# Attention in a two-layer encoder: division and transposes of a unit one turn later, values two turns later, convolution products moved into later stages

## The chip, the core and the metric

The kernel runs on one core of one Trainium2 chip. The metric is device microseconds (us) of one launch; lower is better. Engines are called by their names: TensorE (PE in the profile; its weight loads are PEld), VectorE (DVE), ScalarE (ACT), GpSimd (POOL) and SyncE (SP), which issues most of the loads.

## The reference

What is computed is an encoder of two layers over a prompt of 512 tokens and a sample of 256 tokens, D = 1024. Each layer is a gated feed-forward part, a mixer, and a second feed-forward part, each followed by a scaled residual and a layer norm. The mixer has one input projection, and two head groups that read it: a windowed attention and a long convolution (Hyena). Cut to the mixer:

```python
z = h @ w_in[l]
q, k, v, hz = jnp.split(z, [D_ATTN, D_ATTN + KV_WIDTH, D_ATTN + 2 * KV_WIDTH], axis=-1)
...
def _window_attention(q, k, v, sink):          # blocks of 128 queries, own block and both neighbours as keys
    s = jnp.einsum('bnqkgd,bnskd->bnkgqs', qb, kb) * (HEAD_DIM ** -0.5)
    s = jnp.where(valid[None, :, None, None], s, -jnp.inf)
    m = jnp.maximum(s.max(-1, keepdims=True), sink_f)
    p = jnp.exp(s - m)
    p = p / (p.sum(-1, keepdims=True) + jnp.exp(sink_f - m))
    o = jnp.einsum('bnkgqs,bnskd->bnqkgd', p.astype(v.dtype), vb)
...
def _bidir_long_conv(u, filt, bias):
    U = jnp.fft.rfft(uf, n=2 * L, axis=1)
    K = jnp.fft.rfft(kern, n=2 * L, axis=0)
    y = jnp.fft.irfft(U * K[None], n=2 * L, axis=1)[:, :L]
...
x <- LN_b(alpha*x + (1+g2)*W_out[RMS(attn_group) | RMS(hyena_group)])
```

There are 8 query heads and 2 key heads of 64, so each key head serves a group of 4 query heads. A block of 128 queries sees two key blocks where it is at an end of its sequence, and three otherwise.

## The kernel before, in words

**Precision and memory.** Every large product is three TensorE products of a high and a low part: high by high, high by low, low by high. Splitting takes a copy (mostly ScalarE, which rounds to the high part) and a subtraction (VectorE, the low part). Buffers are drawn in turn from pools (`SLOTS`, L120): `slot_s` 10, `slot_w` 6, `slot_r` 7, `slot_t` 6, `bank` 8 (the accumulators of TensorE), `tiny` 12. An instruction waits until the last reader of the buffer that it takes over is done.

**Order.** Each engine does its instructions in the order in which the Python code issues them; nothing reorders them later. All of them pass through one recording helper, `call` (L67, its body L70), so every row of the profile says L70, and an instruction is known by its tiles.

**The mixer of a layer** (`run`, L1371). `proj.unit(n)` (L444) is one unit of the input projection, 4 to 11 here. Between them stands the convolution, in two halves of the channels (`hy0`, `hy1`; class `Hyena`, L1275 to L1323). For each half: `u_transposes` (L1244) turns the gated input, `u_spectrum` (L1257) multiplies it with a DFT matrix (36 matmuls, six banks that ScalarE copies out), `products(a)` (L1283) for the thirds a = 0, 1, 2 multiplies with the filter's spectrum on VectorE with splits on ScalarE, `inverse(a)` (L1307) goes back with 24 matmuls, and `gate(a)` (L1321) multiplies the result into `x0` on VectorE. Then come three passes g = 0, 1, 2 over two query groups and the keys with the values, three steps each: 48 matmuls, the transposes of the step before, then on ScalarE and VectorE the rotary step and the splits. After each of the nine steps `side(3 * g + tp)` (L1405) issues pieces of other work: rest of the convolution, the group norm of its output (`Rms`, L1325: squares, stats, bcast, apply), and the start of attention.

**Attention** (`Attention`, L1513). Its work is 12 units, a block of queries times a group of 4 heads: units 0 to 3 the sample's, 4 to 11 the prompt's. Units 6 to 9 have three key blocks (384 columns a head), the others two (256). A unit goes through

- `scores` (L1526): 8 matmuls into banks; VectorE adds the mask and takes the row maxima, one instruction a head, into `slot_w`;
- `exps` (L1552): ScalarE, four exponentials with row sums, and one small one for the sink term;
- `norms` (L1562): VectorE adds the sink term, forms the reciprocal, and divides two heads; ScalarE divides the other two;
- `turned` (L1575): TensorE transposes the probabilities, one bank per key block, and ScalarE copies each bank out as the high part; `turned_lo` (L1588): VectorE forms the low parts (the second parts) from the same banks;
- `values` (L1592): 6 or 9 matmuls, then a ScalarE copy into `oT`.

The loop in `attention` (L1652) runs over turns u = 1 to 12. Unit 0 and the scores and exponentials of unit 1 are issued ahead of it by `side`. Within a turn also stand: `filler` (L1636, 12 in all, 12 matmuls each, the hyena half of the output projection, and its addition to the residual on VectorE), `block_squares` (L1620, a ScalarE square and two VectorE sums for a finished block, for the group norm), and the group norm of the sample. `Out` (L489) takes the output projection's weights; its `ahead` says how many units of weights are split before their turn.

Of the kernel before, what the change touches and what calls it, by code (L numbers as in the profile page):

```python
# [160 lines left out]
def _program(mem, nc, x_in, c_col, c_row, w_units, ada_nat, ada_t, ada_b, ln_p, conv_p, sink_in, grp_in,  # L161
# [1025 lines left out]
    def mixer(l, x_prev, hh, hl):  # L1187
# [183 lines left out]
        def run(end):  # L1371
# [10 lines left out]
            proj.unit(8)  # L1382
            hy0.inverse(0, dinv)
            u_transposes(1)
            hy0.products(2)
            proj.unit(9)
            hy0.gate(0)
            hy0.inverse(1, dinv)
            hy1 = Hyena(1, u_spectrum(1, dfw))
            hy0.gate(1)  # L1390
            hy0.inverse(2, dinv)
            hy1.products(0)
            proj.unit(10)
            hy0.gate(2)
            hy1.products(1)
            proj.unit(11)
            hy1.inverse(0, dinv)
            hy1.products(2)
            hy1.gate(0)

            rms = [Rms(x0[0], 4, s) for s in range(2)]
            on_hy = []
            att = []

            def side(i):  # L1405
                if i == 0:
                    hy1.inverse(1, dinv)
                    hy1.gate(1)
                elif i == 1:
                    hy1.inverse(2, dinv)  # L1410
                    hy1.gate(2)
                    rms[0].squares()
                elif i == 2:
                    rms[1].squares()
                elif i == 3:
                    for r in rms:
# [188 lines left out]
        def attention(at, rms, on_hy, last_q, end):  # L1605
# [14 lines left out]
            def block_squares(qb):  # L1620

                if not Q:
                    Q.append(slot_t([T]))
                cols = slice(qb * P, (qb + 1) * P)
                sq = slot_t([4, P])
                act.activation(out=sq, in_=oT[:, :, cols], func=AF.Square)
                tt(sq[:, 0:2], sq[:, 0:2], sq[:, 2:4], ALU.add)
                tt(Q[0][:, cols], sq[:, 0], sq[:, 1], ALU.add)
# [1 line left out]
            oT = slot_s([4, T])  # L1630
            o_hy = Out([on_parts(on_hy, k) for k in range(4)])
            fill = [(d, ks) for d in range(6) for ks in ((0, 1), (2, 3))]
            share = (0, 0, 1, 1, 1, 1, 1, 1, 1, 1, 1, 2)
            fbank = {}

            def filler():  # L1636
# [12 lines left out]

            on_at, done = [], []  # L1650
            rms_at = [Rms(oT, 0, s) for s in range(2)]
            for u in range(1, 13):  # L1652
                if 1 < u < 12:
                    at.scores(u)
                if u > 1:
                    at.turned(u - 1)
                    if u < 12:
                        at.exps(u)
                else:
                    filler()  # L1660
                    last_q()
                if u > 1:
                    at.turned_lo(u - 1)
                if done:
                    block_squares(done.pop())
                if u == 1:
                    rms[0].apply(on_hy, (2, 3))
                elif u == 2:
                    rms[1].apply(on_hy, (2, 3))
                    reload()  # L1670
                elif u == 6:
                    rms_at[1].Q = Q[0][:, SEQ[1]]
                    rms_at[1].stats()
                elif u == 7:
                    rms_at[1].bcast()
                    on_at.append(slot_s([2, 2, T], F32R))
                elif u == 8:
                    rms_at[1].apply(on_at, (0, 1))
                elif u == 11:
                    on_at.append(slot_s([2, 2, T], F32R))  # L1680
                    rms_at[1].apply(on_at, (2, 3))
                adds = [filler() for _ in range(share[u - 1])]
                if u < 12:
                    at.norms(u)
                for add in adds:
                    add()
                at.values(u - 1, oT)
                if at.units[u - 1][1]:
                    done.append(at.units[u - 1][0])
            block_squares(done.pop())  # L1690
            while fill:
                filler()()
# [233 lines left out]
```

## Time and profile before

| what | value |
|---|---|
| median of 3 runs | 2940.02 us (2939.73 to 2941.28) |
| the profiled execution's own time | 2938.19 us |
| its span in the trace | 2936.2 us |
| mean granted TensorE clock, of full speed | 0.987 |
| busy TensorE, matmuls (PE) | 2837.5 us, 97% of the span |
| busy TensorE, weight loads (PEld) | 2594.4 us, 88% |
| busy VectorE | 2139.2 us, 73% |
| busy ScalarE | 1367.5 us, 47% |
| busy GpSimd | 331.8 us, 11% |
| mean DMA rate | 124 GB/s |

Busy shares are averages over the whole launch, feed-forward parts and mixers together. A mean says nothing of a stage: the mixer of layer 0 lies at about 700 to 960 us of the span, its attention loop at about 863 to 950. The full speed of TensorE's clock is 2.4 GHz, and the lower level 1.2 GHz; a granted clock between 0.5 and 1 is a mean over a stretch with both.

### The profile page before, as it was taken

Reading aid. Unit: us, or ns where it says so; the run is one execution under the profiler, and the core shown is the slowest. Engines: PE = TensorE matmul, PEld = TensorE weight load, DVE = VectorE, ACT = ScalarE, POOL = GpSimd, SP = SyncE. Lnnn points to the kernel's source line nnn. Section 1 sums busy time; section 2 is a strip of 40 time slices with the busy share of each in tenths; the row PEclk is TensorE's granted clock in tenths of the full one; section 3 lists DMA queues with packets and bytes.
Section 4 is the critical chain, followed back from the end, with each engine's and each line's share of the span. In section 5 each row is a group of like instructions: output and inputs, shape, how many; then the busy total and the mean of one; then the engine's idle time right before and its main releaser. Section 6 shows DMA issues by size and latency. Waiting matters only on the chain. (4 is left out here: it accounts for less than half of the span.)

```text
span 2936.2 us, 42164 instructions
## 1 busy us (share of the span) xinstructions
PE 2837.5 (97%) x16468; PEld 2594.4 (88%) x16468; DVE 2139.2 (73%) x3821; ACT 1367.5 (47%) x2355; POOL 331.8 (11%) x394
## 2 busy tenths in 40 slices
PE   9999999999998999999999999999999899999998
PEld 3789999988887889999988999998888788999997
DVE  5788778878967887777588777557896787444558
ACT  3544444444366544444445444444436644444444
POOL 2400000031000300000030000002100030000000
PEclk9999999999999999999999999999999999999999
DMA  5546665542121135664333665344212112455332
GB/s 202 194 171 173 188 176 164 147 151 103 57 73 51 65 127 161 194 194 116 107 122 122 179 176 157 107 107 145 102 63 73 51 57 89 85 115 115 97 108 83
DMA packets 102607, 364.65 MB, mean 124 GB/s; under 512 B 13750, under 2 KB 17031, under 8 KB 99208
## 3 DMA queue, kind: packets, MB, share of 16 engines
q1 hardware_dynamic: 74968, 259.88, 24.5%
q0 software_dynamic: 27440, 102.08, 16.2%
q8 instruction: 129, 2.11, 0.3%
q14 instruction: 70, 0.57, 0.1%
HBM read 284.33 MB, written 80.74 MB: 124 GB/s over the span
## 5 line engine op out<-in xcount | busy, mean ns | idle before, releaser
L70 PE MATMUL bank<-slot_s,slot_w 128*128 128x384 f32 (+2 forms) x13176 | 2322.1, 336 | 44.0 <-DVE slot_s L70 26.7
L70 PEld LDWEIGHTS bank<-slot_s,slot_w 128*128 128x128 f32 x13176 | 2130.5, 190 | 212.2 <-DVE slot_s L70 23.0
L70 DVE TENSOR_TENSOR slot_w<-slot_w,slot_w 128x1024 fp32r<-128x1024 f32 (+2 forms) x444 | 370.0, 864 | 4.1 <-ACT slot_w L70 1.6
L70 DVE CUSTOM_DVE_ANT_0 slot_t<-slot_r,slot_r 128x1024 bf16<-128x1024 f32 x256 | 311.4, 1223 | 77.4 <-DMA x_spill<-slot_t 45.0
L70 ACT ACTIVATE slot_w<-slot_w 128x1024 fp32r<-128x1024 f32 (+1 forms) x298 | 249.7, 838 | 119.2 <-DVE slot_w L70 118.9
L70 DVE TENSOR_TENSOR slot_w<-slot_r,slot_w 128x1024 fp32r<-128x1024 f32 (+1 forms) x194 | 222.0, 1153 | 113.4 <-ACT slot_w L70 111.9
L70 ACT ACTIVATE slot_t<-bank,tiny 128x512 f32<-128x512 f32 (+1 forms) x256 | 147.5, 580 | 307.9 <-PE bank L70 302.1
L70 POOL DMA_DIRECT2D x_spill<-slot_t x128 | 110.4, 862 | 1409.2 <-ACT slot_t L70 1409.2
L70 ACT ACTIVATE slot_w<-slot_r 128x1024 fp32r<-128x1024 f32 (+1 forms) x194 | 189.0, 992 | 155.9 <-DVE slot_r L70 98.1
L70 ACT ACTIVATE slot_t<-slot_t 128x384 f32<-128x384 f32 (+2 forms) x161 | 84.1, 526 | 334.2 <-DVE slot_t L70 334.0
L70 DVE TENSOR_TENSOR slot_t<-bank,slot_t 128x384 f32<-128x384 f32 x228 | 125.5, 555 | 144.2 <-PE bank L70 73.5
L70 DVE TENSOR_TENSOR slot_s<-slot_t,slot_s 128x768 fp32r<-128x768 f32 (+2 forms) x190 | 153.1, 810 | 52.6 <-ACT slot_s L70 48.4
L70 ACT ACTIVATE slot_s<-slot_t 128x768 fp32r<-128x768 f32 (+2 forms) x160 | 113.8, 717 | 159.9 <-DVE slot_t L70 155.5
L70 ACT ACTIVATE slot_t<-bank 128x384 f32<-128x384 f32 (+3 forms) x282 | 139.6, 495 | 101.6 <-PE bank L70 99.1
L70 PE MATMUL bank<-slot_s,slot_r 128*128 128x384 f32 x912 | 172.0, 337 | 0.0
L70 PEld LDWEIGHTS bank<-slot_s,slot_r 128*128 128x128 f32 x912 | 160.6, 188 | 0.0
L70 DVE TENSOR_TENSOR slot_r<-slot_w,slot_r 128x512 fp32r<-128x512 f32 x76 | 52.0, 684 | 106.4 <-ACT slot_r L70 106.4
L70 ACT ACTIVATE slot_t<-slot_s 128x256 f32<-128x256 f32 (+1 forms) x132 | 65.9, 510 | 108.0 <-DVE slot_s L70 104.1
L70 PE MATMUL bank<-slot_w,slot_s 128*128 128x256 f32 x864 | 107.9, 284 | 3.1 <-DVE slot_w L70 1.8
L70 PEld LDWEIGHTS bank<-slot_w,slot_s 128*128 128x128 f32 x864 | 104.7, 191 | 3.9 <-DVE slot_w L70 2.1
L70 DVE SCALAR_TENSOR_TENSOR slot_t<-bank,slot_t 128x384 f32<-128x384 f32 x76 | 42.3, 556 | 83.4 <-PE bank L70 82.2
L70 DVE SCALAR_TENSOR_TENSOR slot_s<-bank,tiny,slot_s 128x256 f32<-128x256 f32 (+1 forms) x160 | 87.0, 564 | 15.1 <-PE bank L70 14.9
(137 smaller groups left out, 2132.2 us busy)
## 6 DMA issues: line engine op xcount, KB each, us to landing
slot_r<-w_units SPq DMA_DIRECT2D x170, 512.0 KB, 4.8
slot_w<-w_units SPq DMA_DIRECT2D x146, 512.0 KB, 4.1
slot_r<-ada_t SPq DMA_DIRECT2D x128, 512.0 KB, 5.8
x_spill<-slot_t POOLq DMA_DIRECT2D x128, 384.0 KB, 5.3
slot_s<-x_spill POOLq DMA_DIRECT2D x12, 1536.0 KB, 8.2
x_spill<-slot_s POOLq DMA_DIRECT2D x10, 1024.0 KB, 4.6
slot_r<-ada_nat SPq DMA_DIRECT2D x16, 512.0 KB, 5.9
g_main<-slot_s POOLq DMA_DIRECT2D x4, 1536.0 KB, 10.0
```

The lines of the kernel that those rows point to most:

```text
L70: return getattr(real, name)(*args, **kwargs)
```

## The change

The attention loop gets 13 turns in place of 12. In turn u it issues: scores (and maxima) of unit u, `norms` of u-1, exponentials of u, other work, fillers, `values` of u-2, `turned` of u-1, the fillers' additions, `block_squares`, and last `turned_lo` of u-1. Before, turn u had scores of u, `turned` of u-1, exponentials of u, `turned_lo` of u-1, `block_squares`, other work, fillers, `norms` of u, additions, `values` of u-1. The group norm of the sample moves by one turn, both applications of the hyena group norm stand at u = 1, and `o_hy.ahead` is 1 in place of 2. In the convolution, `hy0.products(2)`, the units 10 and 11 of the projection, and the second half's inverses, last products and gates are placed anew, some of them into `side` 0 to 2. No instruction's shape is changed.

```diff
@@ run, convolution @@
             u_transposes(1)
-            hy0.products(2)
             proj.unit(9)
             hy0.gate(0)
             hy0.inverse(1, dinv)
             hy1 = Hyena(1, u_spectrum(1, dfw))
             hy0.gate(1)
+            hy0.products(2)
+            proj.unit(10)
+            hy1.products(0)
+            proj.unit(11)
             hy0.inverse(2, dinv)
-            hy1.products(0)
-            proj.unit(10)
             hy0.gate(2)
             hy1.products(1)
-            proj.unit(11)
-            hy1.inverse(0, dinv)
-            hy1.products(2)
-            hy1.gate(0)
...
             def side(i):
                 if i == 0:
+                    hy1.inverse(0, dinv)
+                    hy1.gate(0)
+                elif i == 1:
                     hy1.inverse(1, dinv)
+                    hy1.products(2)
                     hy1.gate(1)
-                elif i == 1:
+                    rms[0].squares()
+                elif i == 2:
                     hy1.inverse(2, dinv)
                     hy1.gate(2)
-                    rms[0].squares()
-                elif i == 2:
                     rms[1].squares()
...
@@ attention @@
-            share = (0, 0, 1, 1, 1, 1, 1, 1, 1, 1, 1, 2)
+            share = (1, 0) + (1,) * 11
...
-            for u in range(1, 13):
+            o_hy.ahead = 1
+            for u in range(1, 14):
                 if 1 < u < 12:
                     at.scores(u)
-                if u > 1:
-                    at.turned(u - 1)
-                    if u < 12:
-                        at.exps(u)
-                else:
-                    filler()
+                if u == 1:
                     last_q()
-                if u > 1:
-                    at.turned_lo(u - 1)
-                if done:
-                    block_squares(done.pop())
-                if u == 1:
-                    rms[0].apply(on_hy, (2, 3))
-                elif u == 2:
-                    rms[1].apply(on_hy, (2, 3))
+                    for r in rms:
+                        r.apply(on_hy, (2, 3))
+                elif u < 13:
+                    at.norms(u - 1)
+                if 1 < u < 12:
+                    at.exps(u)
+                if u == 2:
                     reload()
...
                 adds = [filler() for _ in range(share[u - 1])]
-                if u < 12:
-                    at.norms(u)
+                if u > 1:
+                    at.values(u - 2, oT)
+                if 1 < u < 13:
+                    at.turned(u - 1)
                 for add in adds:
                     add()
-                at.values(u - 1, oT)
-                if at.units[u - 1][1]:
-                    done.append(at.units[u - 1][0])
+                if done:
+                    block_squares(done.pop())
+                if u > 1 and at.units[u - 2][1]:
+                    done.append(at.units[u - 2][0])
+                if 1 < u < 13:
+                    at.turned_lo(u - 1)
```

**ScalarE in the turn of unit 8 (three key blocks), before.** `slot_w` with 384 columns are the probabilities: `slot_w_1092` those of unit 7, `slot_w_1108` those of unit 8. `x4` are exponentials, `x2` a division of two heads, `64x4x128` a copy of values, and `slot_r<-bank` copies of transposed probabilities:

```order
L70 ACTIVATE slot_w_1092_8087<-slot_w_1092_8087,tiny_1093_8088 128x384 x2
L70 ACTIVATE slot_s_1021_7674<-bank_1107_8165 64x4x128
L70 ACTIVATE slot_r_1115_8202<-bank_1114_8197 128x512
L70 ACTIVATE slot_r_1117_8209<-bank_1116_8204 128x512
L70 ACTIVATE slot_r_1119_8216<-bank_1118_8211 128x512
L70 ACTIVATE slot_w_1108_8176,tiny_1109_8177<-slot_w_1108_8176,tiny_1109_8177 128x384 x4
...
L70 ACTIVATE slot_w_1108_8176<-slot_w_1108_8176,tiny_1109_8177 128x384 x2
```

The same place after the change, where `slot_w_1087` is unit 7 and `slot_w_1102` unit 8:

```order
L70 ACTIVATE slot_w_1087_8061<-slot_w_1087_8061,tiny_1088_8062 128x384 x2
L70 ACTIVATE slot_w_1102_8146,tiny_1103_8147<-slot_w_1102_8146,tiny_1103_8147 128x384 x4
...
L70 ACTIVATE slot_s_1021_7674<-bank_1112_8196 64x4x128
L70 ACTIVATE slot_r_1114_8212<-bank_1113_8207 128x512
L70 ACTIVATE slot_r_1116_8219<-bank_1115_8214 128x512
L70 ACTIVATE slot_r_1118_8226<-bank_1117_8221 128x512
L70 ACTIVATE slot_t_1119_8228<-slot_s_1021_7674 128x512
L70 ACTIVATE slot_w_1102_8146<-slot_w_1102_8146,tiny_1103_8147 128x384 x2
```

Behind the division of unit 7 now stand at once the exponentials of unit 8; the copy of values (now those of unit 6), the three copies of the transposed unit 7 and, in this turn, a square come after them, where the copies stood ahead of them.

**VectorE in the same turn, before.** `RECIPROCAL` and `x2` are the division, `ISA` with `mask` a row maximum of one head (three more are left out), `slot_r<-bank,slot_r` the low parts of the transposed unit:

```order
L70 TENSOR_TENSOR tiny_1093_8088<-tiny_1093_8088 128x4
L70 RECIPROCAL tiny_1093_8088<-tiny_1093_8088 128x4
L70 TENSOR_SCALAR slot_w_1092_8087<-slot_w_1092_8087,tiny_1093_8088 128x384 x2
L70 SCALAR_TENSOR_TENSOR slot_s_1018_7669<-bank_1087_8054,tiny_1020_7672,slot_s_1018_7669 128x512
L70 SCALAR_TENSOR_TENSOR slot_s_1018_7669<-bank_1088_8055,tiny_1020_7672,slot_s_1018_7669 128x256
L70 ISA slot_w_1108_8176,tiny_1109_8177<-bank_1110_8178,mask 128x384
...
L70 TENSOR_TENSOR slot_r_1115_8202<-bank_1114_8197,slot_r_1115_8202 128x512
L70 TENSOR_TENSOR slot_r_1117_8209<-bank_1116_8204,slot_r_1117_8209 128x512
L70 TENSOR_TENSOR slot_r_1119_8216<-bank_1118_8211,slot_r_1119_8216 128x512
...
L70 TENSOR_TENSOR tiny_1109_8177<-tiny_1109_8177 128x4
L70 RECIPROCAL tiny_1109_8177<-tiny_1109_8177 128x4
L70 TENSOR_SCALAR slot_w_1108_8176<-slot_w_1108_8176,tiny_1109_8177 128x384 x2
```

After the change:

```order
L70 ISA slot_w_1102_8146,tiny_1103_8147<-bank_1104_8148,mask 128x384
...
L70 TENSOR_TENSOR tiny_1088_8062<-tiny_1088_8062 128x4
L70 RECIPROCAL tiny_1088_8062<-tiny_1088_8062 128x4
L70 TENSOR_SCALAR slot_w_1087_8061<-slot_w_1087_8061,tiny_1088_8062 128x384 x2
L70 TENSOR_TENSOR slot_t_1119_8228<-slot_t_1119_8228 128x256
L70 TENSOR_TENSOR slot_t_1069_7975<-slot_t_1119_8228 128x128
L70 TENSOR_TENSOR slot_r_1114_8212<-bank_1113_8207,slot_r_1114_8212 128x512
L70 TENSOR_TENSOR slot_r_1116_8219<-bank_1115_8214,slot_r_1116_8219 128x512
L70 TENSOR_TENSOR slot_r_1118_8226<-bank_1117_8221,slot_r_1118_8226 128x512
L70 ISA slot_w_1120_8235,tiny_1121_8236<-bank_1122_8237,mask 128x384
```

Before, the division of unit 7 stands ahead of the maxima of unit 8, and the low parts of unit 7 behind them. After, the maxima of unit 8 come first, then the division of unit 7, the sums of a square and the low parts of unit 7, and only then the maxima of unit 9 (`slot_w_1120`).

## Rows read from the trace of the kernel before

Columns are explained with the first group of each view. In the timeline, "idle" is the engine's time without work just before the instruction, and the name behind the arrow is what ended it.

**Rows 1.** Windows of 20 us, layer 0: busy PE, PEld, DVE, ACT, POOL; PEclk, DMA, GB/s.
```profile
860.00:880.00 20.00, 16.48 (x86) 13.41 (x85) 16.58 (x56) 15.93 (x45) 0.00 (x0) 0.83 0.05 19
...
900.00:920.00 20.00, 16.79 (x98) 14.27 (x99) 17.33 (x61) 15.59 (x39) 0.00 (x0) 1.00 0.01 2
```

**Rows 2.** Timeline, convolution, layer 0: start, us, engine, operation, [idle before it <- releaser].
```profile
751.02 0.68 DVE L70 TENSOR_TENSOR slot_r<-slot_r,slot_s 128x512 f32<-128x512 f32 x1
...
752.04 3.04 PE L70 MATMUL bank<-slot_s,slot_w 128*128 128x256 f32 x24
...
754.88 1.47 DVE L70 TENSOR_TENSOR slot_w<-slot_r,slot_w 128x512 fp32r<-128x512 f32 x2
...
759.43 2.53 PE L70 MATMUL bank<-slot_s,slot_w 128*128 128x256 f32 x12 [4.34 <-DVE slot_s L70]
...
765.31 16.84 PE L70 MATMUL bank<-slot_s,slot_w 128*128 128x512 f32 x96
...
796.56 0.47 DVE L70 TENSOR_TENSOR slot_t<-bank,rope 128x32 f32<-128x32 f32 x4
...
797.70 0.90 DVE L70 TENSOR_TENSOR slot_r<-slot_t,slot_r 128x128 fp32r<-128x128 f32 x4 [0.44 <-ACT slot_r L70]
...
801.42 0.81 PE L70 MATMUL bank<-ident,slot_r 128*128 128x128 f32 x8
```

**Rows 3.** Timeline, one turn of attention with three key blocks, DVE and ACT.
```profile
907.77 0.15 DVE L70 TENSOR_TENSOR tiny<-tiny 128x4 f32<-128x4 f32 x1
...
908.23 1.12 ACT L70 ACTIVATE slot_w<-slot_w,tiny 128x384 f32<-128x384 f32 x2 [1.17 <-DVE tiny L70]
...
909.26 0.57 ACT L70 ACTIVATE slot_s<-bank 64x512 f32<-64x512 f32 x1
...
909.89 0.55 DVE L70 CUSTOM_DVE_ANT_0 slot_w<-bank,mask 128x384 f32<-128x384 f32 x1
...
910.33 1.58 ACT L70 ACTIVATE slot_r<-bank 128x512 fp32r<-128x512 f32 x3 [0.49 <-PE bank L70]
...
912.26 1.88 DVE L70 TENSOR_TENSOR slot_r<-bank,slot_r 128x512 fp32r<-128x512 f32 x3
...
912.38 0.62 ACT L70 ACTIVATE slot_w<-slot_w,tiny 128x384 f32<-128x384 f32 x1 [0.47 <-DVE tiny L70]
...
914.79 0.19 ACT L70 ACTIVATE tiny<-tiny 128x4 f32<-128x4 f32 x1
```

**Rows 4.** Timeline, one turn with two key blocks, DVE and ACT.
```profile
872.63 0.91 ACT L70 ACTIVATE slot_w<-slot_w,tiny 128x256 f32<-128x256 f32 x2 [0.87 <-DVE tiny L70]
...
873.11 0.42 DVE L70 CUSTOM_DVE_ANT_0 slot_w<-bank,mask 128x256 f32<-128x256 f32 x1
...
874.95 1.28 DVE L70 TENSOR_TENSOR slot_r<-bank,slot_r 128x512 fp32r<-128x512 f32 x2
...
876.99 0.19 ACT L70 ACTIVATE tiny<-tiny 128x4 f32<-128x4 f32 x1
```

**Rows 5.** Timeline, a square, its sums and a weight split in other turns.
```profile
883.18 0.62 ACT L70 ACTIVATE slot_t<-slot_s 128x512 f32<-128x512 f32 x1
...
883.83 0.75 DVE L70 TENSOR_TENSOR slot_t<-slot_t 128x256 f32<-128x256 f32 x2 [1.50 <-ACT slot_t L70]
...
897.79 1.04 ACT L70 ACTIVATE slot_w<-slot_r 128x1024 fp32r<-128x1024 f32 x1
```

**Rows 6.** Timeline, DVE: the reciprocals of units 1 and 11, the first and last of eleven.
```profile
865.75 0.18 DVE L70 RECIPROCAL tiny<-tiny 128x4 f32<-128x4 f32 x1
...
940.78 0.18 DVE L70 RECIPROCAL tiny<-tiny 128x4 f32<-128x4 f32 x1
```

**Rows 7.** Timeline, PE: two waits ahead of transposes in attention.
```profile
866.46 1.94 PE L70 MATMUL bank<-ident,slot_w 128*128 128x128 f32 x8 [3.05 <-DVE slot_w L70]
...
900.98 1.00 PE L70 MATMUL bank<-ident,slot_w 128*128 128x128 f32 x4 [2.17 <-DVE slot_w L70]
```

**Rows 8.** Timeline, PE: the wait for weights after attention.
```profile
953.31 1.93 PE L70 MATMUL bank<-slot_s,slot_w 128*128 128x256 f32 x14 [0.76 <-DVE slot_w L70]
```

More of the change, by code (lines that the diff above doesn't have):

```diff
@@ L1651, in attention @@
             rms_at = [Rms(oT, 0, s) for s in range(2)]
-            for u in range(1, 13):
+            o_hy.ahead = 1
+            for u in range(1, 14):
                 if 1 < u < 12:
                     at.scores(u)
-                if u > 1:
-                    at.turned(u - 1)
-                    if u < 12:
-                        at.exps(u)
-                else:
-                    filler()
-                    last_q()
-                if u > 1:
-                    at.turned_lo(u - 1)
-                if done:
-                    block_squares(done.pop())
-                if u == 1:
-                    rms[0].apply(on_hy, (2, 3))
-                elif u == 2:
-                    rms[1].apply(on_hy, (2, 3))
+                if u == 1:
+                    last_q()
+                    for r in rms:
[5 more added lines that the diff above has]
+                if u == 2:
                     reload()
-                elif u == 6:
+                elif u == 7:
                     rms_at[1].Q = Q[0][:, SEQ[1]]
                     rms_at[1].stats()
-                elif u == 7:
+                elif u == 8:
                     rms_at[1].bcast()
                     on_at.append(slot_s([2, 2, T], F32R))
-                elif u == 8:
+                elif u == 9:
                     rms_at[1].apply(on_at, (0, 1))
-                elif u == 11:
+                elif u == 12:
                     on_at.append(slot_s([2, 2, T], F32R))
```

## The prediction

> **What bounds the kernel now.** I read the totals first: TensorE is busy for 97% of the span, VectorE for 73%, ScalarE for 47%. Then the busy time by stretches of 20 us: TensorE is full in the feed-forward parts and has its holes in the two mixers. In the attention stretch it works 16.5 and 16.8 us of 20, beside 16 to 17 us of VectorE and 16 us of ScalarE [rows 1]: no engine is full, so the stretch is held by a chain that runs from engine to engine. Then the timeline of the two places that the change touches, in layer 0 (layer 1 shows the same holes some 1,395 us later).
>
> *Convolution.* TensorE stops for 4.34 us at 759.4 [rows 2] in the middle of the spectrum of the second half: the ScalarE copies that free its banks stand behind the copies of `products(2)`, which wait for VectorE. VectorE has no gap from there to the rotary step of the first key pass at 796.56 [rows 2].
>
> *Attention.* One turn with three key blocks goes like this [rows 3]: VectorE adds the sink term at 907.77, ScalarE divides two heads from 908.23, copies the last values at 909.26 and the transposed probabilities at 910.33, VectorE takes the maxima from 909.89 to 912.26, ScalarE the exponentials from 912.38 to 914.98, and the next division follows at once, or after a square or a group norm. VectorE's second parts at 912.26 lie beside the exponentials. The loop that closes is division, maxima, exponentials. From the reciprocal of unit 1 to that of unit 11 there are ten turns in 75.03 us [rows 6].
>
> **The change, part by part.** Durations are those of one profiled execution, 2938.19 us with a span of 2936.2 us; the median of the runs is 1.83 us above it, and I add that at the end. No instruction is added or removed on any engine; only order, and with it tile reuse, changes.
>
> *1. The loop of a turn, the large term.* In the new order ScalarE has: division of unit u-1, exponentials of u, copy of the values of u-2, copies of the turned u-1, square. VectorE has: maxima of u, division of u-1, additions, square sums, second parts of u-1, and only then the maxima of u+1. The second parts need ScalarE's copies, the copies stand behind the exponentials of u, and those need the maxima of u. So everything that lay beside the exponentials is now in one closed loop, which I add up from rows, each duration as the step to the next instruction on its engine.
> With three blocks [rows 3]: maxima 2.37 (909.89 to 912.26), to ScalarE 0.46 (907.77 to 908.23), division 1.03, exponentials 2.50, values copy 0.55, three copies 1.58, last second part 0.65: **9.14 us**. With two blocks [rows 4]: maxima 1.84 (873.11 to 874.95), 0.46, division 0.81 (0.91 less the 0.1 by which neighbours on ScalarE overlap), exponentials 2.08 (from 875.0 to 877.1), 0.55, two copies 1.09 (two thirds of 1.58 and a start), 0.65: **7.48 us**. Where a square falls in the turn, VectorE's square sums wait for ScalarE's square and stand ahead of the second parts, which then can't follow the copies one by one: the copies (1.50 or 1.00), square 0.62, 0.04, sums 0.67, all second parts 1.80 or 1.20 [rows 3, 5] replace the last two terms, which gives **11.54** and **9.27**. A weight split on ScalarE adds 0.95 [rows 5].
> The ten turns u = 2 to 11: four plain ones of two blocks (2, 3, 4, 11) 29.92; u=5 with a square 9.27; u=6, maxima of three blocks but a division of two, with square and split, 11.17; u=7 9.14; u=8 with square 11.54; u=9, where the group norm of the sample adds about 1.2, 10.35; u=10, two and three blocks with square and split, 11.54. Sum 92.93, against 75.03: **+17.9**. The maxima of unit 2 start at about 865.2, 0.4 before the old division of unit 1, and from the end of turn 11 to the last values matmul I count 7.9 us (division, turned copies, square, second parts, values) where there were 8.85: -1.35. TensorE's own work in the three-block turn of that timeline (scores 1.58, transposes 1.53, filler 2.35, values 2.25: 7.7 us) fits into the loop and costs nothing more; if its clock fell, see the second rival. Attention: **+16.55 per layer**.
>
> *2. Weights after attention.* With one split ahead in place of two, the first unit of the attention half of the output projection is split only behind the last values copy and the last square. Copy 0.6, square 0.6, ScalarE's split 1.05 and VectorE's 1.2 make about 3.5 us before its third matmul; now TensorE runs on and waits 0.76 one unit later [rows 8]. The second unit then starts about 6.6 us after the values in place of 3.87: **+2.7 per layer**. Bounds: 0, if the wait is eaten by a later one that stands anyway, and 4.4, if the clock falls in it.
>
> *3. Products later.* VectorE's queue up to the rotary step loses `products(2)` of the second half, 5.35 us like its twin (751.02 to 756.35 [rows 2]), and a gate of 0.65; the queue is full, but it now comes to unit 10's convolution about 2 us before TensorE has finished that unit (8.4 us, half of 16.84 [rows 2]). So the rotary step moves from 796.56 to about 792.5, and the transposes that follow it 2.05 us later (796.56 to 798.60) are ready at 794.5. TensorE, without the old hole, ends the spectrum at 756.6 (36 matmuls from 752.04 at 3.04 us for 24), and with two units 16.84, two inverses of 3.04 and two key passes of 6.1 it is there at 791.7 and waits. In place of 801.42 less the inverse of 3.0 us that it still owes, that is **-3.9 per layer**. Bounds: -6.7, if it does not wait, and 0. `products(2)` and its inverse now stand in the key passes, where VectorE waits for TensorE again; I cost them at nothing, and at 3 us if the inverse of that third has to wait for them.
>
> *4. Queues.* SP's loads keep their order and come tens of us before use; POOL moves one small power. Filler matmuls, 12 as before, one per turn: nothing.
>
> Sum per layer: 16.55 + 2.7 - 3.9 = 15.35; two layers 30.7. 2938.19 + 30.7 + 1.83 = **2971 us**.
>
> **Rivals.** *Slower still: the clock.* In the loop TensorE waits twice a turn, mostly 1.7 to 2 us, but about 3.05 us in u=8, where scores of unit 9 need banks that the second parts of unit 7 still hold. Before, a wait of 2.17 us left the clock at its upper level (1.00 in that stretch), and one of 3.05 us was followed by the lower one: 0.83 as the mean of its 20 us [rows 1, 7]. If it falls in most of the turns 6 to 10, their TensorE work of 7.7 us takes up to 15.4 and becomes the bound: 5 x 15.4 = 77 for 53.7, so up to 23 us per layer, 3017 us at the end. Against it: one fall costs only 2 or 3 us, and part of that is idle anyway. The Trainium skill ("TensorE: Matmul & The Clock Gate", section "A second HAM failure mode: psum-queue depth-cycling") says that TensorE can swing between its levels where it idles briefly between groups of matmuls as it cycles through banks; by that rule the time would be this rival's, and the trace, where a 2.17 us wait did nothing, agrees only for the longer wait.
>
> *Faster: TensorE is the bound.* If dividing a unit late really took ScalarE and VectorE off the path, a turn would last as long as TensorE's own work: scores, transposes, filler and values, 6.1 us with two blocks and 7.7 with three, 67.4 for the ten turns, -7.6; with the whole 6.7 from the convolution 14.3 per layer, **2911 us**. For it: the new order asks for values two turns after the scores. Against it: it needs the copies of u-1 ahead of the exponentials of u on ScalarE, or the maxima of u+1 ahead of the second parts of u-1 on VectorE, and both stand the other way. It would decide as soon as ScalarE's wait for the maxima were gone.
>
> *No change.* The convolution gives 6.7 and attention costs no more: it would need turns of about 8.3 us on average, which only holds if the squares' extra 2 us in five turns, the rest of the copies and the weight wait all vanish: 2940 us.
>
> **Numbers.** Forecast 0.76 (range of its own 2951 to 2992: -6.7, no weight wait and 4.5 us less in the turns at the one end; 0, 4.4 and two clock falls of 2.5 us per layer at the other). Clock rival 0.10, faster 0.08, no change 0.06. I give 2950 to 2994, which leaves out the faster case, no change and the greater part of the clock case. A change under 0.2% (5.9 us) can't be told from none by these runs. Slower: 0.86, same 0.05, faster 0.09.
>
> **What would show it.** In the new trace the ten turns from the maxima of unit 2 to those of unit 12's place should take 90 to 97 us; ScalarE should wait for VectorE ahead of each division and each exponential, and VectorE for ScalarE ahead of the second parts, with TensorE's waits on VectorE's second parts in each turn. The hole at 759 should be gone and a shorter one stand ahead of the transposes of the first key pass. The forecast is wrong if the turns come out near 7 us, or if the second parts of a unit start before the exponentials of the next have ended.

## The result, and the profile after

The changed kernel takes **2973.2 us** (median of 4 runs, 2971.89 to 2974.78) against 2939.88 us before: a ratio of 1.0116, 95% interval 1.0098 to 1.0133. The forecast was 2971 us. The profiled execution took 2971.89 us with a span of 2969.7 us, 33.5 us more than the span before.

The windows of the changed kernel come first: two of 20 us that answer to [rows 1], then the turns of units 3, 6 and 8, each from its first row maximum to the next unit's, and last 5 us behind attention. Columns as in [rows 1].

```profile
860.00:880.00 20.00, 16.61 (x91) 13.40 (x90) 10.79 (x47) 12.39 (x40) 0.00 (x0) 0.91 0.08 27
900.00:920.00 20.00, 15.83 (x79) 12.43 (x79) 11.96 (x41) 11.52 (x31) 0.71 (x1) 0.91 0.00 1
...
866.65:874.11 7.46, 5.72 (x27) 4.53 (x26) 4.97 (x20) 4.42 (x14) 0.00 (x0) 0.79 0.00 0
891.28:902.33 11.05, 6.17 (x25) 4.63 (x23) 6.32 (x22) 6.30 (x16) 0.00 (x0) 0.82 0.00 0
911.85:923.24 11.39, 7.24 (x37) 5.40 (x36) 5.82 (x22) 6.05 (x16) 0.00 (x0) 0.95 0.00 1
...
965.00:970.00 5.00, 5.00 (x25) 5.00 (x25) 2.54 (x5) 0.61 (x2) 0.40 (x1) 0.51 0.88 286
```

VectorE and ScalarE, at 16 to 17 us of 20 before, are down to 11 or 12, and TensorE has not filled the room. No engine is full, which fits three engines that wait for each other in a closed chain; the timeline shows the waits. In the turn of unit 8 TensorE works 7.2 of 11.4 us.

The timeline of the changed kernel, in order of time: the convolution, the turn of unit 3 (two key blocks), the turn of unit 8 (three blocks and a square), and the start of the weights behind attention.

```profile
744.10 2.44 DVE L70 SCALAR_TENSOR_TENSOR slot_s<-bank,convp,slot_s 128x511 f32<-128x511 f32 x4
...
749.26 21.16 PE L70 MATMUL bank<-slot_s,slot_w 128*128 128x256 f32 x132
...
789.22 0.48 DVE L70 TENSOR_TENSOR slot_t<-bank,rope 128x32 f32<-128x32 f32 x4
...
790.58 1.19 PE L70 MATMUL bank<-ident,slot_r 128*128 128x128 f32 x8 [1.66 <-ACT slot_r L70]
...
866.65 0.41 DVE L70 CUSTOM_DVE_ANT_0 slot_w<-bank,mask 128x256 f32<-128x256 f32 x1
...
868.95 1.31 ACT L70 ACTIVATE slot_w<-slot_w,tiny 128x256 f32<-128x256 f32 x3 [3.06 <-DVE tiny L70]
...
872.30 1.06 ACT L70 ACTIVATE slot_r<-bank 128x512 fp32r<-128x512 f32 x2
...
872.91 1.29 DVE L70 TENSOR_TENSOR slot_r<-bank,slot_r 128x512 fp32r<-128x512 f32 x2 [2.35 <-ACT slot_r L70]
...
874.11 0.41 DVE L70 CUSTOM_DVE_ANT_0 slot_w<-bank,mask 128x256 f32<-128x256 f32 x1
...
914.68 1.63 ACT L70 ACTIVATE slot_w<-slot_w,tiny 128x384 f32<-128x384 f32 x3 [3.70 <-DVE tiny L70]
...
918.68 1.54 ACT L70 ACTIVATE slot_r<-bank 128x512 fp32r<-128x512 f32 x3
...
920.11 0.63 ACT L70 ACTIVATE slot_t<-slot_s 128x512 f32<-128x512 f32 x1
920.77 0.75 DVE L70 TENSOR_TENSOR slot_t<-slot_t 128x256 f32<-128x256 f32 x2 [5.39 <-ACT slot_t L70]
921.44 1.88 DVE L70 TENSOR_TENSOR slot_r<-bank,slot_r 128x512 fp32r<-128x512 f32 x3
922.18 1.65 PE L70 MATMUL bank<-slot_s,slot_s 128*128 128x384 f32 x4 [2.74 <-DVE slot_r L70]
...
962.51 0.50 PE L70 MATMUL bank<-slot_s,slot_w 128*128 128x256 f32 x2 [2.29 <-ACT slot_w L70]
963.77 8.47 PE L70 MATMUL bank<-slot_s,slot_w 128*128 128x256 f32 x46 [0.76 <-DVE slot_w L70]
```

*Convolution.* The 4.34 us hole of [rows 2] is gone: TensorE runs through the spectrum and the two units behind it without a wait (749.26; 36 and 96 matmuls). The first rotary step stands at 789.22 in place of 796.56, and a shorter wait, 1.66 us, now stands ahead of the transposes behind it.

*A turn.* ScalarE waits 3.06 us for VectorE's maxima and reciprocal (868.95; the row holds two divisions and the first exponential), does division, exponentials and one copy of values, and copies the transposed unit only at 872.30. VectorE, idle for 2.35 us, can start the second parts only then, and behind them come the next maxima, 7.46 us after the last. In the turn of unit 8, VectorE waits 5.39 us, because the sums of the square wait for ScalarE's square at 920.11 and the second parts stand behind them; TensorE waits 2.74 us at 922.18 for banks that those second parts hold.

*Behind attention.* TensorE stops for 2.29 and 0.76 us at 962.51 and 963.77 for weights, where 0.76 us stood in [rows 8], and its granted clock from 965 to 970 is 0.51.

### The profile page after: what moved, and what is told of

Its sections match the earlier page's. It is cut to its first block, busy times and chain, and to the rows that moved or that the text cites. A ratio compares the mean times of both kernels' runs of the same rounds, so it can differ in the third digit from the quotient of the medians.

```text
span 2969.7 us, 42163 instructions
## 1 busy us (share of the span) xinstructions
PE 2851.7 (96%) x16468; PEld 2603.9 (88%) x16468; DVE 2139.3 (72%) x3821; ACT 1365.8 (46%) x2355; POOL 332.2 (11%) x394
## 5 line engine op out<-in xcount | busy, mean ns | idle before, releaser
L70 ACT ACTIVATE slot_w<-slot_w,tiny 128x256 f32<-128x256 f32 (+1 forms) x144 | 72.4, 533 | 82.5 <-DVE tiny L70 82.5
```

Source lines behind the costliest of these rows:

```text
L70: return getattr(real, name)(*args, **kwargs)
```

## The experiments

Each kernel ran on a chip beside the kernel before. The medians of the kernel before differ by up to 2.2 us from chip to chip, so a difference between two kernels from two chips is uncertain by as much. In the table, "ten turns" are the times between the reciprocals of units 1 and 11 in layer 0 of the profiled execution (as [rows 6]).

| kernel | median us | before, us | ratio, 95% interval | ten turns, us |
|---|---|---|---|---|
| before | 2939.88 | | | 75.03 |
| changed | 2973.2 | 2939.88 | 1.0116, 1.0098 to 1.0133 | 92.12 |
| conv_only | 2933.01 | 2939.24 | 0.9979, 0.9969 to 0.9988 | 76.22 |
| attn_only | 2977.5 | 2939.24 | 1.0135, 1.0120 to 1.0150 | 92.12 |
| squares_last | 2958.36 | 2939.24 | 1.0068, 1.0053 to 1.0083 | 87.19 |
| copies_first_sq | 2941.06 | 2939.24 | 1.0004, 0.9995 to 1.0014 | 76.77 |
| maxima_first | 2948.94 | 2937.7 | 1.0039, 1.0024 to 1.0054 | 77.14 |
| ahead_two | 2968.91 | 2937.7 | 1.0103, 1.0087 to 1.0120 | 92.14 |
| copies_split_sq | 2919.53 | 2937.7 | 0.9940, 0.9925 to 0.9955 | 66.79 |
| best1 | 2918.23 | 2937.7 | 0.9933, 0.9918 to 0.9948 | 69.04 |
| ahead_late | 2919.91 | 2939.2 | 0.9934, 0.9922 to 0.9947 | 71.80 |
| start_early | 2916.0 | 2939.2 | 0.9927, 0.9914 to 0.9941 | 75.58 |
| weights_early | 2913.77 | 2938.2 | 0.9909, 0.9896 to 0.9923 | 66.80 |
| both_ends | 2910.23 | 2938.2 | 0.9904, 0.9891 to 0.9918 | 71.89 |

(In start_early and both_ends the division of unit 1 stands a turn earlier, so their ten turns hold part of the start.)

### The two parts apart: conv_only and attn_only

conv_only is the attention loop of before with the new placement of products, inverses and gates; attn_only is the reverse: every `-` and `+` of the diff's first part, or of its second part, undone.

> The attention loop of before with the convolution order of the change. Theory (the two parts add up; in the trace after the change the rotary step and the key passes of layer 0 come about 3.1 us earlier than before): 2 x 3.1 us less than before, about 2934 us. Rival 1 (the forecast's -3.9 per layer holds and the new loop hid a part): about 2932. Rival 2 (attention starts no earlier, because something else holds its start): 2940. In the trace the 4.3 us hole in the spectrum of the second half should be gone.

> The convolution order of before with the attention loop of the change. Theory (the loop is closed within itself, so an earlier or later start only shifts it): 6 us more than the changed kernel, about 2979 us, with the same turns of 7.5 to 11.9 us between reciprocals. Rival (the two parts interact: the moved inverses and products disturb the key passes and the start of attention, so that undoing them gives nothing or a gain): 2973 or less.

conv_only took 6.2 us less than before and attn_only 4.3 us more than the changed kernel (2977.5 to 2973.2). The turns of attn_only are those of the changed kernel to 0.1 us. The intervals of the changed kernel and attn_only overlap, but the traces agree: from the row that stands at 744.10 in the changed kernel to the first reciprocal, layer 0 takes 107.49 us with the old convolution order (before, attn_only) and 104.31 with the new one (conv_only, changed). So the parts add: the convolution gives some 3 us per layer, and the attention loop costs some 19 per layer (38.3 us more than before in attn_only). The 76.22 us of conv_only come from layer 0 alone, where one turn took 8.62 us in place of 7.76 at a granted clock of 0.60, and the next 8.56 in place of 8.23; in layer 1 its ten turns take 75.04.

### The order inside the loop: squares_last

```diff
+                if 1 < u < 13:
+                    at.turned_lo(u - 1)
                 if done:
                     block_squares(done.pop())
                 if u > 1 and at.units[u - 2][1]:
                     done.append(at.units[u - 2][0])
-                if 1 < u < 13:
-                    at.turned_lo(u - 1)
```

> The changed kernel, with the block squares issued behind the second parts in place of ahead of them. Theory (a turn is the closed loop over maxima, division, exponentials, copies and second parts; a square's sums ahead of the second parts make these wait for ScalarE's square): the square turns fall by 1.7 us (three blocks) or 1.1 us (two blocks), five turns, 6.7 us per layer, so about 2960 us. Rival (TensorE at a lowered clock holds the turns): no change, 2973.

14.8 us less than the changed kernel. Only the square turns moved: 9.95, 11.04, 11.39 and 11.88 us between reciprocals became 8.94, 10.21, 9.91 and 10.28, and the plain turns of units 2 and 3 stayed at 7.47 and 7.48 us. One square turn, that of unit 5, from its first row maximum to the next unit's:

```profile
881.67 0.41 DVE L70 CUSTOM_DVE_ANT_0 slot_w<-bank,mask 128x256 f32<-128x256 f32 x1
...
888.21 1.29 DVE L70 TENSOR_TENSOR slot_r<-bank,slot_r 128x512 fp32r<-128x512 f32 x2 [2.63 <-ACT slot_r L70]
889.42 0.74 DVE L70 TENSOR_TENSOR slot_t<-slot_t 128x256 f32<-128x256 f32 x2
890.08 0.55 DVE L70 CUSTOM_DVE_ANT_0 slot_w<-bank,mask 128x384 f32<-128x384 f32 x1
```

The second parts no longer wait for the square, and the sums (889.42) find it done. But the sums still stand ahead of the next maxima: this turn takes 8.41 us where a plain one takes 7.47. So the wait has left the loop, and the sums have not. The rival, with no change, falls.

### Opening the loop on ScalarE: copies_first_sq

squares_last, and the exponentials of u issued behind the copies:

```diff
                 elif u < 13:
                     at.norms(u - 1)
-                if 1 < u < 12:
-                    at.exps(u)
...
                 if 1 < u < 13:
                     at.turned(u - 1)
+                if 1 < u < 12:
+                    at.exps(u)
```

> The changed kernel, with two edits: on ScalarE the copies of values and of the turned unit u-1 are issued ahead of the exponentials of u, and the block squares behind the second parts. Theory (the loop runs through the copies that stand behind the exponentials): the loop becomes maxima 2.37, 0.46, division 1.03, transposes 0.6, copies 1.58, second part 0.65, 6.7 us with three blocks, less than TensorE's own 7.7, so TensorE is the bound: ten turns in about 67 us in place of 92.1, some 25 us less per layer, about 2924 us, faster than both kernels. Rival 1 (the division a turn late is itself the cost, whatever the order of copies): no more than the squares give, 2960. Rival 2 (the clock: TensorE's gaps still lower it, turns of up to 10 us): 2950 or more.

It took 2941.06 us, 32 less than the changed kernel where 49 were expected. Its timeline, one plain turn and the end of the square turn of unit 8:

```profile
864.88 1.09 ACT L70 ACTIVATE slot_r<-bank 128x512 fp32r<-128x512 f32 x2
...
865.52 1.29 DVE L70 TENSOR_TENSOR slot_r<-bank,slot_r 128x512 fp32r<-128x512 f32 x2 [1.40 <-ACT slot_r L70]
865.86 0.51 ACT L70 ACTIVATE slot_w<-slot_w,tiny 128x256 f32<-128x256 f32 x1
...
866.72 0.41 DVE L70 CUSTOM_DVE_ANT_0 slot_w<-bank,mask 128x256 f32<-128x256 f32 x1
...
913.06 0.63 ACT L70 ACTIVATE slot_t<-slot_s 128x512 f32<-128x512 f32 x1
...
913.72 0.75 DVE L70 TENSOR_TENSOR slot_t<-slot_t 128x256 f32<-128x256 f32 x2 [2.09 <-ACT slot_t L70]
914.39 0.55 DVE L70 CUSTOM_DVE_ANT_0 slot_w<-bank,mask 128x384 f32<-128x384 f32 x1
```

In the plain turn the second parts (865.52) lie beside the exponentials (from 865.86), and the next maxima follow at 866.72: the turn takes 5.46 us, and TensorE shows no wait through the two turns behind it. In the square turn the square on ScalarE now stands behind the exponentials, the sums wait for it until 913.72, and the maxima stand behind the sums: 8.8 to 10.1 us in four turns. My expectation had left this second chain out. One turn without a square is long too, that of unit 7, here in layer 0 and in layer 1 (columns as in [rows 1]):

```profile
898.52:907.13 8.61, 8.61 (x51) 7.81 (x50) 6.74 (x23) 5.76 (x15) 0.71 (x1) 0.90 0.01 2
2296.63:2306.15 9.52, 9.52 (x52) 8.52 (x51) 6.73 (x22) 5.76 (x15) 0.71 (x1) 0.84 0.00 0
```

TensorE is busy through all of it, with the clock at 0.90 and 0.84; in copies_split_sq below the same turn takes 7.05 us at 1.00, with 45 matmul records. So rival 2, the clock, has a share here, together with matmuls left over from the turn before. Rival 1 falls, since the plain turns are a quarter shorter than in squares_last with the same late division.

### Opening it on VectorE instead: maxima_first

```diff
                 elif u < 13:
                     at.norms(u - 1)
+                if u > 2:
+                    at.turned_lo(u - 2)
...
-                if 1 < u < 13:
-                    at.turned_lo(u - 1)
...
-            share = (1, 0) + (1,) * 11
+            share = (1, 0, 1, 1, 1, 1, 1, 0, 1, 1, 1, 1, 2)
```

> The changed kernel, with the second parts of unit u-1 issued behind the maxima and the division's first half of the next turn in place of ahead of its maxima; one filler is moved from turn 8 to the last turn, since the eight banks don't hold it there. Theory (the loop is closed because the maxima of u+1 stand behind the second parts of u-1): without that place the loop loses the maxima, plain turns fall to TensorE's own 5.5 to 6 us, while in the square turns the sums still hold the maxima (8 to 10.7 us): ten turns in about 78 us in place of 92.1, 14 us less per layer, about 2945 us. Rival 1 (it is the order on ScalarE alone that counts): no gain, 2973. Rival 2 (banks held longer make TensorE wait): a gain of half that or less, 2960 to 2973.

11.2 us over its own before, and 24 less than the changed kernel, with ten turns in 77.14 us, near the theory's 78. A plain turn takes 6.33 us, a little over the 5.5 to 6 expected. In its timeline TensorE now feeds the maxima:

```profile
875.02 0.42 DVE L70 CUSTOM_DVE_ANT_0 slot_w<-bank,mask 128x256 f32<-128x256 f32 x1 [2.26 <-PE bank L70]
...
877.81 1.28 DVE L70 TENSOR_TENSOR slot_r<-bank,slot_r 128x512 fp32r<-128x512 f32 x2
878.55 1.42 PE L70 MATMUL bank<-slot_r,slot_t 128*128 128x512 f32 x5 [0.77 <-DVE slot_r L70]
```

VectorE waits for scores and not for ScalarE, and TensorE waits 0.77 us for second parts that come a turn later.

### Both, with the square in two: copies_split_sq

The changed kernel with copies first; the square's ScalarE part goes to the head of the turn, its sums behind the second parts:

```diff
                     at.scores(u)
+                sums = block_squares(done.pop()) if done else None
...
-                if done:
-                    block_squares(done.pop())
...
                     at.turned_lo(u - 1)
+                if sums:
+                    sums()
```

> The changed kernel with ScalarE's copies ahead of the exponentials, and the squares in two: ScalarE's square at the head of a turn, where it waits for the maxima anyway, VectorE's sums behind the second parts. Theory (copies_first_sq was held in five turns by the square behind the exponentials, and elsewhere by TensorE, which shows no waits in turns of 5.46 us with two blocks and 7.4 us with three): ten turns in about 63 us in place of 76.8, 14 us less per layer than that kernel: about 2912 us. Rival (the turns with three blocks are held by something else, the clock after TensorE's waits or banks): 2925 to 2941.

2919.53 us, 53.7 less than the changed kernel and 0.6% faster than before (0.9925 to 0.9955). The turns are 5.47, 5.46, 5.69, 6.88, 7.73, 7.05, 7.65, 7.45, 8.22 and 5.19 us, 66.79 in all against the 63 expected. In the turns of units 3, 4, 5, 7, 8 and 9 TensorE is busy from end to end at a clock of 1.00; in those of units 6 and 10, 7.73 and 8.22 us, it is busy for 5.45 and 7.42. Layer 1 took 68.23, all of the difference in one turn of 6.90 us. Windows of layer 1, for the turns of units 2 and 3:

```profile
2253.80:2259.30 5.50, 4.77 (x22) 4.11 (x23) 3.94 (x18) 4.46 (x14) 0.00 (x0) 0.70 0.01 3
2259.30:2266.20 6.90, 6.90 (x45) 6.20 (x44) 4.97 (x20) 4.53 (x14) 0.00 (x0) 0.99 0.00 0
```

The clock fell to a mean of 0.70 in the first, with 22 matmul records there and 45 in the next, which TensorE filled to the end. Layer 0 had 1.00 in both places. So here, where TensorE is what the turn waits for, a fall cost time.

### The weights: ahead_two, best1 and ahead_late

```diff
-            o_hy.ahead = 1
```

> The changed kernel with two weight units split ahead, as before the change, in place of one. Theory (one split ahead costs 2.7 us per layer after attention, as forecast): about 2968 us. Rival 1 (the wait is eaten later): 2973. Rival 2 (the split that is taken earlier falls into the closed loop on ScalarE and gives 0.95 us of it back): 2970.

4.3 us less than the changed kernel, near the theory; the two intervals overlap, but in the traces both terms show, and both were larger. The start grew: 14.54 us between the first two reciprocals, where the changed kernel has 12.79. The end gave more: from the reciprocal of unit 11 to the VectorE row at 985.49 of the changed kernel there are 27.81 us in place of 32.17. The granted clock behind attention, where the changed kernel showed 0.51:

```profile
967.00:972.00 5.00, 5.00 (x45) 5.00 (x44) 3.99 (x9) 2.18 (x4) 0.40 (x1) 1.00 0.65 213
```

45 matmul records in 5 us, where the changed kernel has 25.

best1 is copies_split_sq with two ahead from the start and the first filler ahead of the transposes of the last query group (`adds = [filler()]` ahead of `last_q()`).

> The kernel before this one, with two more edits: the first filler is issued ahead of the transposes of the last query group, where TensorE waits 2.8 us in the changed kernel, and two weight units are split ahead. Theory (the first wait is covered, and 2.6 us per layer of the weights' wait goes): 2 x (1.4 + 2.6) us less than the kernel before this one, about 2904 us if that one takes 2912. Rival (the start hangs on the last query group's chain, not on TensorE, and the earlier split costs ScalarE as much): no gain over it.

It took 2918.23 us, no gain that these runs can tell: 14.89 us between the first two reciprocals against 13.21, and the turns of units 2 and 3 grew to 6.02 and 7.17. What the end gave went back at the start, as its rival had it, and the clock has a share in that: its mean was 0.50 in the turn of unit 2, where copies_split_sq has 1.00 in the same layer. Which of the two edits costs how much was not tried apart.

ahead_late is copies_split_sq with `o_hy.ahead = 2` and `w_ahead(2)` at the end of turn 4.

> The kernel copies_split_sq with the second weight unit split ahead only from turn 4 on, in place of at the start or never. Theory (in the run with two ahead from the start, the split at the start cost 1.74 us between the first two reciprocals and the wait after attention gave 3.9 us per layer; so a split in a turn where ScalarE has room gives nearly all of it): 2 x 3.9 us less, less at most 0.5 us per turn and layer, about 2912 us where copies_split_sq took 2919.5. Rival (the split lengthens the turn in which it stands as much as the start): about 2915. Second rival (the wait after attention is eaten by a later one): 2919.

2919.91 us: no gain. That is the second rival's time, but not its reason, since the wait behind attention is gone (0.74 us is left); the first rival's mechanism, with a higher price, took the gain: the end is 3.2 us per layer shorter than in copies_split_sq, and turn 4 is 3.4 longer. The split's place in its timeline:

```profile
880.99 1.06 ACT L70 ACTIVATE slot_w<-slot_r 128x1024 fp32r<-128x1024 f32 x1
...
882.08 1.23 DVE L70 TENSOR_TENSOR slot_w<-slot_r,slot_w 128x1024 fp32r<-128x1024 f32 x1 [2.20 <-ACT slot_w L70]
883.23 0.42 DVE L70 CUSTOM_DVE_ANT_0 slot_w<-bank,mask 128x256 f32<-128x256 f32 x1
```

VectorE's half of the split waits 2.20 us for ScalarE's, which stands behind the exponentials, and the maxima of unit 5 wait behind it: that turn took 9.13 us where copies_split_sq took 5.69.

### The start and the end: start_early, weights_early and both_ends

start_early is ahead_late with the first filler ahead of `last_q()`, `at.norms(1)` in turn 1, and the second group norm's application behind turn 2.

> The kernel ahead_late with an earlier start: the first filler ahead of the transposes of the last query group, the division of unit 1 in turn 1 (as before the change) and the second application of the hyena group norm behind turn 2. Theory (in the changed kernel the start is held by VectorE: the maxima of unit 2 and the division of unit 1 stand behind two applications of the group norm, 12.8 us between the first two reciprocals where there were 11.4): 1 to 1.5 us per layer less, about 2909 us. Rival (the chain of the last query group, split, transposes, copies, scores of unit 2, holds the start whatever stands beside it): no gain over ahead_late.

weights_early is copies_split_sq with one edit at the end of a turn, behind the second parts and the sums; both_ends has the same edit in place of the split in turn 4 of start_early.

```diff
+                if u == 12:
+                    w_ahead(2)
```

> The kernel copies_split_sq with the second weight unit split at the end of turn 12, behind the second parts of unit 11 and ahead of the last values copy and square (in the run before it stood in turn 4, which grew from 6.9 to 9.1 us, because VectorE's half of the split stood ahead of the next maxima). Theory (ScalarE and VectorE have nothing else there while TensorE does the last values, so the wait of 2.29 us and the lowered clock behind it go at no price): 3.5 to 4 us less per layer, about 2912 us where copies_split_sq took 2919.5. Rival (the split delays the last values copy, and with it the squares and the group norm, by as much): 2917 to 2920.

> The kernel start_early with its weight split moved from turn 4 to the end of turn 12 as in weights_early. Theory (start and end add: the start gave some 1.3 us per layer between the first and the third reciprocal): about 2 to 3 us less than weights_early, 2909 us. Rival (the start's gain is taken up by the third turn, which waits for the second group norm's parts): no gain over weights_early.

start_early took 3.9 us less than ahead_late and both_ends 3.5 less than weights_early. The intervals of each pair overlap, but the gain came twice, each time a little more than expected. weights_early took 5.8 us less than copies_split_sq; in its trace the end is 2.9 us shorter in each layer, against 3.5 to 4 expected, and the ten turns take 66.80 us, as long as there. (The turn that its expectation puts at 6.9 us is that of unit 4, which took 5.69 in copies_split_sq.) The end of attention in both_ends:

```profile
931.25 1.06 ACT L70 ACTIVATE slot_w<-slot_r 128x1024 fp32r<-128x1024 f32 x1
...
932.77 1.22 DVE L70 TENSOR_TENSOR slot_w<-slot_r,slot_w 128x1024 fp32r<-128x1024 f32 x1
...
934.04 3.14 PE L70 MATMUL bank<-slot_s,slot_w 128*128 128x256 f32 x24 [0.46 <-DVE slot_w L70]
```

The split lies beside TensorE's last values, and the waits of 2.29 and 0.76 us are down to 0.46 and, one group later, 0.30. **both_ends** is faster than both kernels: 2910.23 us, 0.9904 of before (0.9891 to 0.9918).

## Why the prediction was right

The forecast was 2971 us and the median is 2973.2. Its terms, in layer 0, stand below beside what the two traces show. The entry into the mixer came 2.78 us earlier in the changed kernel's execution (a VectorE row at 746.88 before stands at 744.10), with the same code ahead of it; in the other traces of this case that row lies between 741.43 and 747.84, so the 2.78 is taken out here as scatter. The rows that bound the terms, first before, then after:

```profile
854.37 0.18 DVE L70 RECIPROCAL tiny<-tiny 128x4 f32<-128x4 f32 x1
...
865.56 0.15 DVE L70 TENSOR_TENSOR tiny<-tiny 128x4 f32<-128x4 f32 x1
...
947.88 1.56 PE L70 MATMUL bank<-slot_r,slot_t 128*128 128x512 f32 x6
...
970.36 1.23 DVE L70 TENSOR_TENSOR slot_w<-slot_r,slot_w 128x1024 fp32r<-128x1024 f32 x1 [0.80 <-ACT slot_w L70]
```

```profile
848.41 0.18 DVE L70 RECIPROCAL tiny<-tiny 128x4 f32<-128x4 f32 x1
...
859.17 0.42 DVE L70 CUSTOM_DVE_ANT_0 slot_w<-bank,mask 128x256 f32<-128x256 f32 x1
...
953.13 0.15 DVE L70 TENSOR_TENSOR tiny<-tiny 128x4 f32<-128x4 f32 x1
...
958.78 1.44 PE L70 MATMUL bank<-slot_r,slot_t 128*128 128x512 f32 x5 [1.15 <-DVE slot_r L70]
...
985.49 1.23 DVE L70 TENSOR_TENSOR slot_w<-slot_r,slot_w 128x1024 fp32r<-128x1024 f32 x1 [1.21 <-ACT slot_w L70]
```

- **Convolution.** Forecast -3.9. Measured at the reciprocal of unit 0: 848.41 against 854.37, less the 2.78: **-3.2**. For the hole at 759.43 the prediction named ScalarE's copies; [rows 2] names VectorE as what ended the wait, and which of the two frees the bank is not shown. Both stand behind `products(2)`, and the hole is gone.
- **Start.** Forecast -0.4, the maxima of unit 2 against the old division of unit 1 (865.56). From the reciprocal of unit 0 there are 10.76 us in place of 11.19: **-0.4**.
- **Turns.** Forecast 92.93 us from the maxima of unit 2 to the division of unit 11, against 75.03. Measured 859.17 to 953.13, **93.96**. Turn by turn, measured and (forecast), from maxima to maxima: 7.48, 7.46, 7.76 (7.48 each), 9.41 (9.27), 11.05 (11.17), 9.52 (9.14), 11.39 (11.54), 10.31 (10.35), 11.89 (11.54) and 7.7 (7.48). This is the term that carried the forecast, and the chain of durations from rows of before gives each turn within 0.4 us.
- **End of the loop.** Forecast 7.9 us in place of 8.85; measured 953.13 to 960.22 (the last values, 958.78 and 1.44): **7.1**.
- **Weights.** Forecast +2.7, bounds 0 and 4.4. From the end of the last values to a VectorE row 21 us behind it there are 20.9 us before (949.44 to 970.36) and 25.3 after (960.22 to 985.49): **+4.4**. The mechanism was right, and the size was at the upper bound: the wait of 2.29 us that was priced, and the lowered clock behind it that was left to the bound. Here the forecast was furthest off.

Together that is 17.9 us in layer 0, and the row itself says the same (15.13 later, and the 2.78). Between the same two places layer 1 lost 17.6, against 15.35 forecast for each. So the mechanism was right, and the mixers lost 35.5 us where 30.7 were forecast; that the end came within 2.2 us of the forecast is in part luck, since the early entry took 2.8 us back in the profiled execution.

Two of the signs that the prediction named did not come. ScalarE waits for VectorE ahead of each division (38.4 us in the ten turns), but not ahead of the exponentials, which follow the division at once, as the sum itself had it. And TensorE does not wait for the second parts in each turn: its waits for divided probabilities are the longer sum, 8.8 us beside 6.6.

**The rivals.** *The clock.* It did fall: the granted clock was below 1.00 in seven of the ten turns (0.79 to 0.98 as means of a turn). The Trainium skill ("TensorE: Matmul & The Clock Gate", section "A second HAM failure mode: psum-queue depth-cycling") says that TensorE may swing between its levels when it idles briefly between groups of matmuls; for the fall the trace agrees, and the loss of time that the prediction drew from it does not show within the loop. Below stand the turn of unit 5 in layer 0 and in layer 1 (columns as in [rows 1]), and the only wait of VectorE or ScalarE for TensorE that the trace lists in the ten turns, in that of unit 10:

```profile
881.87:891.28 9.41, 7.48 (x35) 6.44 (x34) 5.60 (x22) 5.17 (x15) 0.00 (x0) 0.82 0.00 0
2295.47:2304.89 9.42, 6.38 (x35) 4.87 (x34) 5.60 (x22) 5.17 (x15) 0.00 (x0) 1.00 0.00 1
```

```profile
941.33 1.09 ACT L70 ACTIVATE slot_r<-bank 128x512 fp32r<-128x512 f32 x2 [0.39 <-PE bank L70]
```

The same turn took 9.41 us at 0.82 and 9.42 at 1.00, and no turn differs by more than 0.02 us between the layers. *TensorE as the bound, 2911 us.* The changed kernel is not there, for the reason given: ScalarE's copies and VectorE's second parts stand where they close the loop. Moving the one (copies_first_sq, copies_split_sq) or the other (maxima_first) took 15 to 25 us off the ten turns, in the first two with the squares moved as well (10.4 from squares_last to copies_first_sq, where the squares stand alike), and with the squares out of the way they took 66.8 us, where this rival had 67.4. *No change* would have needed turns of 8.3 us; they were 9.4 on average.

## What to carry to other kernels

To run a stage one unit late helps only if every queue lets it: write down, engine by engine, the order of one turn, and look for a chain that returns to its start. Here two late steps, ScalarE's copies behind the exponentials and VectorE's second parts ahead of the maxima, tied two units together, and moving either opened it. The length of such a loop can be added up from the durations of the old trace, and small extras (a square's sums, half of a weight split) cost a full wait on the other engine if they stand inside it, and less or nothing a few instructions later.

## What the runs showed of the hardware

The same turn of the same kernel, that of unit 3 in copies_split_sq, took 5.46 us in layer 0 and 6.90 in layer 1, with no instruction changed: the granted clock was 1.00 in the one and fell to 0.70 as the mean of the turn before in the other. And a wait of 2.29 us with 0.76 us behind it was followed by 0.51 in the changed kernel, while a wait of 0.76 us at the same place left it at 1.00 in ahead_two. In that turn of unit 3, which TensorE filled, the fall cost 1.4 us; in the turn of unit 5 of the changed kernel, which a loop of the other engines sets, it cost nothing (9.41 us at 0.82, 9.42 at 1.00).
